# Windowed attention in blocks of 64 queries of two heads: narrower score products and a stacked mask product

## The chip, the core and the metric

The kernel runs on one core of a Trainium2 chip. The metric is device microseconds of one execution; the kernel before takes 908.87 us (median of 3 runs, 908.67 to 910.39). The profile is of a further execution, on the same core. Names of engines: TensorE (PE; its weight loads are PEld), VectorE (DVE), ScalarE (ACT), GpSimd (POOL) and SyncE (SP), which issues transfers.

## The reference

One layer of a decoder block on 1024 positions of width 1024: a normalized input goes through one projection whose columns feed an attention branch, a recurrent branch, two gate paths and two merge gates; both branches are gated, projected, merged, projected once more, added to the input and normalized. What the change touches is the attention: 16 heads of width 64, 4 heads per key and value head, each query seeing itself and the 127 positions before it, plus one learned sink per head.

```python
s = jnp.einsum('bnqkgd,bnskd->bnkgqs', qb, kb) * (1.0 / math.sqrt(hd))
diff = qi + BLOCK - kj                       # BLOCK = WINDOW = 128
band = (diff >= 0) & (diff < WINDOW)
s = jnp.where(mask[None, :, None, None], s, -1e30)
m = jnp.maximum(jnp.max(s, axis=-1, keepdims=True), sink)
p = jnp.exp(s - m)
denom = jnp.sum(p, axis=-1, keepdims=True) + jnp.exp(sink - m)
o = jnp.einsum('bnkgqs,bnskd->bnqkgd', p / denom, vb)
```

Everything is float32.

## The kernel before

Nearly all of its time is matmul. A float32 matrix is split into a high part (rounded to the format `F32R`, float32 in TensorE's faster reading) and a low part (the rest); a product is high by high, low by high and high by low, so three matmuls. The projection is done in seven quarter products per pair of output chunks (a Strassen scheme, `Pair` and `run`), and the products, their operand splits and what becomes of their results are put in an order written out by hand (`tc.manual_schedule`, the lists `fixed` and `waiting`, and the costs in tuples such as `("A", 0.62, 0, f1)`). No planner reorders anything: each engine and each queue of transfers runs in the order of the program. The costs in the tuples decide only where background steps are put, and the change leaves them as they are.

*Queries, keys, values.* The projections of queries and keys come out transposed (features on partitions, time along the free dimension), are rotated (`rope_a`) and split by `rope_b`: ScalarE casts the high part (L626), VectorE subtracts it (L630), and both go to memory (`q_d`, `k_d`), 512 positions at a time. `v_prep` reads values, and makes for each group of four heads two arrays: `vs_d`, the values, and `dv_d`, the values of a block of 128 positions minus those of the block before, each as high and low part side by side (128 columns).

*The attention stage* (the loop over u at L1626) goes through 32 blocks: 4 groups of 4 heads, 8 blocks of 128 queries each; block n = u % 8 of group g = u // 8. One iteration interleaves three blocks with pieces of other work (the last projections, then the recurrent branch's output projection, `rp_steps`):

- `scores(u)`: per head j two products of 256 key columns (128 for n = 0). The weights are the 128 queries of head j in `qs` (high part on 64 partitions, low on 64), the moving side the keys `ks` (high, then low): L1274.
- `maxima_a`, `maxima_d`: query row i may see keys i+1 to 127 of the earlier 128 and keys 0 to i of the later 128, which together are 128 places. ScalarE copies the later half (L1282), VectorE puts the earlier half over it where the mask `mgt` holds (L1288), and a maximum is taken (L1293) over 128 places and the sink, which GpSimd has put into column 128 (`sink`, L1262). For n = 0 GpSimd masks instead (L1291).
- `weights_a` and `weights_d` for block u-1: exponentials with sums (L1298), reciprocal and multiplication.
- `values(u-3)`: of a block's transposed probabilities, all go with `vs` of the block before, and what the mask leaves goes with `dv`. The high part `phc`, the low part `plc` and their masked copies `phm`, `plm` make four products of 512 columns (4 heads by 128 queries), two with `dv` alone for n = 0: L1346. `join_a` and `join_d` add the product with the values' high part and that with their low part (L1355 to L1367).
- `transposed(u-2)` (L1312), `split_a` (L1317) and `split_d` (L1323), then `masks(u-2)`: two selects by GpSimd over 4 heads by 128 queries (L1332).

`load_kq` brings keys and queries of two blocks on SP's queue, two pairs of blocks ahead, and waits there until the scores that used the buffer are done. `load_v` brings values of two blocks on GpSimd's queue. Behind the same SP queue stand the loads of gates (`ga_d`), of the recurrent branch's weights (`w_rp`) and states (`yh_d`, `yl_d`), and stores of its results (`tr_d`).

## Time and profile before

| What | Value |
|---|---|
| median of 3 runs | 908.87 us |
| profiled execution, its own time | 909.08 us |
| its span, first to last instruction | 907.4 us |
| granted TensorE clock, mean | 0.999 |
| TensorE busy, weight loads busy | 889.1 us, 739.2 us |
| VectorE, ScalarE, GpSimd busy | 725.8, 554.9, 124.7 us |
| attention stage, 560 to 735 us: TensorE, VectorE, ScalarE, GpSimd busy | 174.53, 153.55, 139.45, 77.34 us |
| transfers | 182.57 MB, 201 GB/s over the span |

Times in the tables of the profile are microseconds from the span's start unless marked ns. A row names the line of the kernel, the engine, the operation, and the tiles as out<-in; a matmul's busy time includes the tail in which the next one already runs, so the distance between starts says what one costs in a stream.

### The profile page before, as it was taken

What the parts mean: (1) busy time and instruction counts of PE and PEld (TensorE: products, weight loads), DVE (VectorE), ACT (ScalarE), POOL (GpSimd) and SP (SyncE); (2) the same over time, 40 slices, a digit from 0 to 9 for tenths busy, and PEclk for the clock granted to TensorE, in tenths of its full rate; (3) what the DMA queues carried; (4) which work ended last, traced back from release to release, by engine and by line L of the source; (5) the groups of instructions that cost most, each with busy time, mean ns of one, the idle gap of its engine ahead of it and who ended that gap; (6) DMA issues with size and microseconds to landing.
All of it is one profiled execution on the core that took longest, in us unless ns stands there. A gap on an engine that the chain in (4) does not pass through costs nothing.

```text
span 907.4 us, 12605 instructions
## 1 busy us (share of the span) xinstructions
PE 889.1 (98%) x4171; PEld 739.2 (81%) x4171; DVE 725.8 (80%) x1158; ACT 554.9 (61%) x1097; POOL 124.7 (14%) x204
## 2 busy tenths in 40 slices
PE   5999999999999999999999999999999999999997
PEld 3879888878888788878887888888888888888885
DVE  7988799698669974987698476899999846779875
ACT  6754675455556745774767685888888731114555
POOL 0120000000110000000100001354443421310002
PEclk9999999999999999999999999999999999999999
DMA  9951786862534360345345257996666258879314
GB/s 348 404 203 68 253 272 223 294 219 97 180 121 151 130 218 24 129 155 180 107 155 183 85 194 254 328 370 211 214 201 212 85 182 322 315 272 346 110 47 186
DMA packets 88882, 182.57 MB, mean 201 GB/s; under 512 B 14049, under 2 KB 30433, under 8 KB 88818
## 3 DMA queue, kind: packets, MB, share of 16 engines
q1 hardware_dynamic: 82192, 162.09, 51.8%
q0 software_dynamic: 6336, 19.37, 5.9%
q8 instruction: 33, 0.54, 0.3%
q10 hardware_dynamic: 290, 0.32, 0.1%
q14 instruction: 31, 0.25, 0.1%
HBM read 125.01 MB, written 57.12 MB: 201 GB/s over the span
## 4 chain that ended last, share of the span: by engine, by line
PE 86%; DVE 6%; DMA 3%; ACT 2%; issue 2%; SPq 0%; POOL 0%; DVEq 0%; ACTq 0%
PE bk L696 41%; PE rp L174 14%; PE bo L1857 7%; PE pmain L174 6%; PE pgate L992 5%; PE s_ps L1274 3%; PE pv L1346 3%; DMA r<-w_main 2%; PE pt L1312 2%; PE bk L174 1%; DVE wl L110 1%; PE bk L1520 1%; PE bk L1519 1%; PE bk L1518 1%; DMA wada<-w_ss 1%
## 5 line engine op out<-in xcount | busy, mean ns | idle before, releaser
L696 PE MATMUL bk<-nh,wl 128*128 128x512 f32 x368 | 143.9, 391 | 0.5 <-DVE wl L110 0.4
L696 PE MATMUL bk<-nh,wh 128*128 128x512 f32 x368 | 143.4, 390 | 0.0
L696 PE MATMUL bk<-nl,wh 128*128 128x512 f32 x368 | 143.2, 389 | 0.0
L696 PEld LDWEIGHTS bk<-nh,wl 128*128 128x128 f32 x368 | 69.1, 188 | 16.7 <-DVE wl L110 2.1
L696 PEld LDWEIGHTS bk<-nh,wh 128*128 128x128 f32 x368 | 69.1, 188 | 14.4 <-ACT rhi L626 0.2
L696 PEld LDWEIGHTS bk<-nl,wh 128*128 128x128 f32 x368 | 69.1, 188 | 14.4
L110 DVE TENSOR_TENSOR wl<-r,wh 128x512 fp32r<-128x512 f32 x112 | 80.1, 729 | 0.0
L60 POOL DMA_DIRECT2D wq_d<-wq x32 | 21.9, 685 | 407.2 <-DVE wq L1172 392.6
L104 ACT CAST wh<-r 128x512 fp32r<-128x512 f32 x112 | 68.0, 617 | 8.8 <-DMA r<-w_ap 5.1
L696 PE MATMUL bk<-hh,wh 128*128 128x512 f32 x184 | 71.6, 389 | 0.0
L696 PE MATMUL bk<-hh,wl 128*128 128x512 f32 x184 | 71.6, 389 | 0.0
L696 PE MATMUL bk<-hl,wh 128*128 128x512 f32 x184 | 71.6, 389 | 0.0
L110 DVE TENSOR_TENSOR wl<-ws,wh 128x512 fp32r<-128x512 f32 x80 | 54.8, 686 | 4.3 <-ACT wh L104 4.2
L104 ACT CAST wh<-ws 128x512 fp32r<-128x512 f32 x80 | 48.2, 614 | 3.3 <-PE bk L1520 2.7
L1298 ACT ACTIVATE p<-p,small 128x129 f32<-128x129 f32 x128 | 50.1, 401 | 0.0
L799 ACT ACTIVATE c<-bk 128x512 f32<-128x512 f32 x31 | 18.5, 595 | 44.0 <-PE bk L696 43.9
L696 PEld LDWEIGHTS bk<-hl,wh 128*128 128x128 f32 x184 | 34.5, 188 | 7.2
L696 PEld LDWEIGHTS bk<-hh,wl 128*128 128x128 f32 x184 | 34.5, 188 | 7.1
L696 PEld LDWEIGHTS bk<-hh,wh 128*128 128x128 f32 x184 | 34.5, 188 | 7.1
L1857 PE MATMUL bo<-wh,sum 128*128 128x512 f32 x128 | 39.6, 389 | 0.0
L1274 PE MATMUL s_ps<-ks,qs 128*128 128x256 f32 (+1 forms) x256 | 37.6, 289 | 0.0
L696 PE MATMUL bk<-hha,wl 128*128 128x512 f32 x92 | 36.1, 393 | 0.6 <-DVE wl L110 0.6
(409 smaller groups left out, 2290.1 us busy)
## 6 DMA issues: line engine op xcount, KB each, us to landing
r<-w_main SPq DMA_DIRECT2D x100, 256.0 KB, 4.3
wada<-w_ss SPq DMA_DIRECT2D x16, 512.5 KB, 9.3
qs<-q_d SPq DMA_DIRECT2D x16, 512.0 KB, 5.8
wq_d<-wq POOLq DMA_DIRECT2D x24, 256.0 KB, 2.8
wr<-wq_d SPq DMA_DIRECT2D x24, 256.0 KB, 5.0
ks<-k_d SPq DMA_DIRECT2D x24, 192.0 KB, 4.2
wq<-w_out POOLq DMA_DIRECT2D x16, 256.0 KB, 5.2
q_d<-rhi SPq DMA_DIRECT2D x16, 256.0 KB, 3.6
```

The lines of the kernel that those rows point to most:

```text
L60: return eng.dma_start(dst, src)
L104: A.copy(dst[0][:], src)
L110: V.tensor_tensor(out=dst[1][:], in0=src, in1=f32(dst[0][:]), op=ALU.subtract)
L174: mm = T.matmul(ps[hf], ww, xx[kc][hf], start=(kc == 0 and ww is w_h and xx is xh), stop=(kc == KC - 1 and xx is xl))
L696: W["pe"] = T.matmul(ps, ww[:, c], b[kc][xx_], start=(first and kc == 0 and i == 0), stop=(kc == 3 and i == 2), skip_group_check=not first)
L799: A.activation(t["t"], s(), AF.Tanh, scale=0.5)
L992: W["pe"] = T.matmul(ps[:, SL[hf]], ww[:, c0:c0 + P], xx_[:, SL[hf]], start=(ic == 0 and i == 0), stop=(ic == 1 and i == 2))
L1274: W["pe"] = T.matmul(o, qs[:, j, qc], ks[:, b, k0 + (0 if n else P):k0 + 256], start=(b == 0), stop=(b == 1))
L1298: A.activation(px[:, j, :], px[:, j, :], AF.Exp, bias=sm[:, 0, j:j + 1], accum_out=sm[:, 1, j:j + 1])
L1312: W["pe"] = T.transpose(pt[:, j, :], px[:, j, 0:P], ident[:])
L1346: W["pe"] = T.matmul(pv[:], b, m[:].rearrange("p j q -> p (j q)"), start=(i == 0), stop=(i == len(prods) - 1))
L1857: T.matmul(bank[p][i] if dst is None else dst, a[:, ts_], b[:][:, sl], start=(new and kc == 0 and j == 0), stop=(kc == 3 and j == 2), skip ...
```

## The change

A block of 128 queries of one head becomes two halves of 64 queries of two heads each.

- *Queries* are stored so that, within 256 positions, position 64 i + q stands at 4 q + i (`turned`, `natural`): the cast and the subtraction in `rope_b` read in the old order and write in the new one. Keys stay as they were.
- *Scores:* the weights of a product are the 64 queries of two heads (half h of the block, heads 0 and 1 or 2 and 3), every fourth element of `qs`; the moving side is the 192 keys that these queries can see (64 or 128 for n = 0). The mask compares within 64 columns, and the predicated copy covers 64 columns of each of four.
- *Values* are stored as 18 half blocks of 64 positions, the first two zero. `load_v` now runs per block, on SP's queue, and brings for each half its earlier 128 positions (`vb`) and the two differences (`vd`), in four transfers, three buffers deep.
- *The value products* take 256 columns each (one half of the queries): high and low probabilities with `vb`, and one product per half with `vd`, whose moving side `cm` holds the masked high part on partitions 0 to 63 and the masked low part on 64 to 127. For n = 0 only the second half has earlier keys.
- *Joins and sinks* follow the new order; the sinks come in two transfers, every second element. At the start GpSimd makes the smaller mask and zeroes the first two half blocks of the values with four transfers.

```diff
@@ -126,8 +126,8 @@
     cs4_d = tc.dram_tile([24, 4, S], F32, name="cs4_d")
     k_d = tc.dram_tile([512, S], F32, name="k_d")
     v_d = tc.dram_tile([P, 8, NG, 64], F32, name="v_d")
-    vs_d = [tc.dram_tile([P, 8, P], F32, name=f"vs_d{g}") for g in range(NG)]
-    dv_d = [tc.dram_tile([P, 8, P], F32, name=f"dv_d{g}") for g in range(NG)]
+    vs_d = [tc.dram_tile([18, 64, P], F32, name=f"vs_d{g}") for g in range(NG)]
+    dv_d = [tc.dram_tile([18, 64, P], F32, name=f"dv_d{g}") for g in range(NG)]
     gate_d = tc.dram_tile([1, D], F32, name="gate_d")
     q_d = [tc.dram_tile([512, S], F32, name=f"q_d{g}") for g in range(NG)]
     ga_d = [tc.dram_tile([2, P, S], F32, name=f"ga_d{g}") for g in range(NG)]
@@ -586,12 +586,18 @@
     ctab = rpp.tile([P, S], F32, name="ctab")
     stab = rpp.tile([64, S], F32, name="stab")
     G.memset(ctab[64:128, :], 1.0)
-    W["mgt"] = const.tile([P, P], U32, name="mgt")
+    W["mle"] = const.tile([P, 64], U32, name="mle")
     mf = rpp.tile([P, HALF], F32, tag="rh", name="mf", bufs=2)[:, :P]
-    G.memset(mf, 1.0)
-    G.affine_select(out=mf, in_=mf, pattern=[[1, P]], compare_op=ALU.is_gt, fill=0.0, base=0,
-                    channel_multiplier=-1)
-    G.tensor_copy(W["mgt"][:], mf)
+    G.memset(mf[:, 0:64], 1.0)
+    for e in range(2):
+        o = mf[64 * e:64 * e + 64, 0:64]
+        G.affine_select(out=o, in_=o, pattern=[[-1, 64]], compare_op=ALU.is_ge, fill=0.0, base=0,
+                        channel_multiplier=1)
+    G.tensor_copy(W["mle"][:], mf[:, 0:64])
+    zero = rpp.tile([P, HALF], F32, tag="rl", name="zero", bufs=2)
+    G.memset(zero[:, :P], 0.0)
+    for g in range(NG):
+        dma(vs_d[g][0:2].rearrange("i r c -> (i r) c"), zero[:, :P], G)
     for b in range(2):
         dma(ctab[b * 32:(b + 1) * 32, :], cs4_d[0:8].rearrange("f j t -> (f j) t"), G)
     dma(stab[0:32, :], cs4_d[16:24].rearrange("f j t -> (f j) t"), G)
@@ -599,6 +605,12 @@
 
     def blk(w=HALF):
         return stp.tile([P, HALF], F32, tag="c", name="c", bufs=5)[:, :w]
+
+    def turned(ap, on):
+        return ap.rearrange("p (b q i) -> p b i q", b=2, i=4) if on else ap
+
+    def natural(ap, on):
+        return ap.rearrange("p (b i q) -> p b i q", b=2, i=4) if on else ap
 
     def rope_a(src, th, dst):
 
@@ -619,15 +631,16 @@
             lambda: t["ra"], th, dst, 0)
 
     def rope_b(src, th, dst, r0=P):
-        t = {}
+        t, q = {}, dst is not k_d
 
         def f1():
             t["h"] = rpp.tile([P, HALF], F32R, tag="rh", name="rhi", bufs=2)
-            A.copy(t["h"][:], src())
+            A.copy(turned(t["h"][:], q), natural(src(), q))
 
         def f2():
             t["l"] = rpp.tile([P, HALF], F32R, tag="rl", name="rlo", bufs=2)
-            V.tensor_tensor(out=t["l"][:], in0=src(), in1=f32(t["h"][:]), op=ALU.subtract)
+            V.tensor_tensor(out=turned(t["l"][:], q), in0=natural(src(), q),
+                            in1=turned(f32(t["h"][:]), q), op=ALU.subtract)
             dma(dst[r0:r0 + P, SL[th]], t["h"][:])
             dma(dst[r0 + 2 * P:r0 + 3 * P, SL[th]], t["l"][:])
 
@@ -1211,7 +1224,7 @@
             for n_, d_, dst in (("v", "vs", vs_d), ("d", "dv", dv_d)):
                 V.tensor_tensor(out=t[d_][:, :, 64:128], in0=t[n_][:],
                                 in1=f32(t[d_][:, :, 0:64]), op=ALU.subtract)
-                dma(dst[g], t[d_][:])
+                dma(dst[g][2:].rearrange("(n b) r c -> (b r) n c", b=2), t[d_][:])
 
         waiting[1].extend(([] if g else [slots(4)]) + [
                            [("S", 0, 0, f0)], slots(4), [("D", 0, 0.85, f1)],
@@ -1227,10 +1240,13 @@
         psm_ctx.close()
         psx = pool(psx_ctx, "psx", space=PSUM)
         at = pool(at_ctx, "at", side="right")
-        W["sink"] = at.tile([P, NH], F32, name="sink")
+        W["sink"] = at.tile([P, NH // 2], F32, name="sink")
         fill_sink = sink(0)
         load_kq(0)
-        dma(W["sink"][:], rows[0:1, D:D + NH].to_broadcast([P, NH]))
+        sinks_ = rows[0:1, D:D + NH].rearrange("o (x e) -> o x e", e=2)
+        for e in range(2):
+            dma(W["sink"][64 * e:64 * e + 64, :],
+                sinks_[:, :, e].to_broadcast([64, NH // 2]))
         fill_sink()
         load_kq(1)
         load_v(0)
@@ -1246,32 +1262,36 @@
         dma(qs[:], q_d[g].rearrange("(a j) t -> a j t", j=4)[:, :, t0:t0 + 256])
         U["kq", m] = ks, qs
 
-    def load_v(m):
-        g, n0 = m // 4, (m % 4) * 2
-        vs = at.tile([P, 2, P], F32R, tag="vs", name="vs", bufs=2)
-        dv = at.tile([P, 2, P], F32R, tag="dv", name="dv", bufs=2)
-        dma(dv[:], dv_d[g][:, n0:n0 + 2, :], G)
-        lo = 0 if n0 else 1
-        dma(vs[:, lo:, :], vs_d[g][:, n0 - 1 + lo:n0 + 1, :], G)
-        U["v", m] = vs, dv
+    def load_v(u):
+        g, i0 = u // 8, u % 8 * 2
+        vb = at.tile([P, 2, P], F32R, tag="vb", name="vb", bufs=3)
+        vd = at.tile([P, 2, P], F32R, tag="vd", name="vd", bufs=3)
+        for e in range(2):
+            half = slice(64 * e, 64 * e + 64)
+            dma(vb[half], vs_d[g][i0 + e:i0 + e + 2].rearrange("i r c -> r i c"))
+            dma(vd[half], dv_d[g][i0 + 2:i0 + 4].rearrange("i r c -> r i c"))
+        U["v", u] = vb, vd
 
     def sink(u):
         px = at.tile([P, 4, P + 1], F32, tag="p", name="p", bufs=3)
         U["p", u] = px, at.tile([P, 2, 4], F32, tag="small", name="small", bufs=4)
-        gs = slice(u // 8 * 4, u // 8 * 4 + 4)
-        return lambda: G.tensor_copy(px[:, :, P:P + 1], W["sink"][:, gs].unsqueeze(2))
+        gs = W["sink"][:, u // 8 * 2:u // 8 * 2 + 2]
+        return lambda: G.tensor_copy(
+            px[:].rearrange("p (h a) k -> p h a k", h=2)[:, :, :, P],
+            gs.unsqueeze(1).to_broadcast([P, 2, 2]))
 
     def scores(u):
         g, n = u // 8, u % 8
         ks, qs = U["kq", u // 2]
-        qc = slice((n % 2) * P, (n % 2 + 1) * P)
-        k0 = (n % 2) * P
         s_full = psx.tile([P, 1024], F32, tag="s", name="s_ps")
         s_ps = s_full[:].rearrange("p (j k) -> p j k", j=4)
         for j in range(4):
-            o = s_ps[:, j, :] if n else s_ps[:, j, P:]
+            h = j // 2
+            t0 = (n % 2) * P + 64 * h
+            first = 0 if n else P - 64 * h
+            w = qs[:].rearrange("p j (q i) -> p (j q) i", i=4)[:, j % 2 * P:j % 2 * P + P, t0 // 64]
             for b in range(2):
-                W["pe"] = T.matmul(o, qs[:, j, qc], ks[:, b, k0 + (0 if n else P):k0 + 256],
+                W["pe"] = T.matmul(s_ps[:, j, first:192], w, ks[:, b, t0 + first:t0 + 192],
                                    start=(b == 0), stop=(b == 1))
         U["s", u] = s_ps, *U.pop(("p", u))
         if n % 2 and u // 2 + 2 < 16:
@@ -1279,17 +1299,25 @@
 
     def maxima_a(u):
         s_ps, px, sm = U["s", u]
-        A.copy(px[:, :, 0:P], s_ps[:, :, P:])
+        if u % 8:
+            A.copy(px[:, :, 0:P], s_ps[:, :, 0:P])
+        else:
+            A.copy(px[:, :, 0:64], s_ps[:, :, P:192])
+            A.copy(px[:, 2:4, 64:P], s_ps[:, 2:4, 64:P])
 
     def maxima_d(u):
         s_ps, px, sm = U["s", u]
-        p = px[:, :, 0:P]
+        p = px[:, :, 0:64]
         if u % 8:
-            V.copy_predicated(p, W["mgt"][:].unsqueeze(1).to_broadcast([P, 4, P]),
-                              s_ps[:, :, 0:P])
+            V.copy_predicated(p, W["mle"][:].unsqueeze(1).to_broadcast([P, 4, 64]),
+                              s_ps[:, :, P:192])
         else:
-            G.affine_select(out=p, in_=p, pattern=[[0, 4], [-1, P]], compare_op=ALU.is_ge,
-                            fill=-1e30, base=0, channel_multiplier=1)
+            G.memset(px[:, 0:2, 64:P], -1e30)
+            for e in range(2):
+                o = p[64 * e:64 * e + 64]
+                G.affine_select(out=o, in_=o, pattern=[[0, 4], [-1, 64]],
+                                compare_op=ALU.is_ge, fill=-1e30, base=0,
+                                channel_multiplier=1)
         V.tensor_reduce(out=sm[:, 0, :], in_=px[:], axis=AX.X, op=ALU.max, negate=True)
 
     def weights_a(u):
@@ -1324,36 +1352,33 @@
         U["m", u] = phc, plc
 
     def masks(u):
-        phc, plc = U["m", u]
-        ms = []
-        if u % 8:
-            for s_, tag in ((phc, "phm"), (plc, "plm")):
-                d_ = at.tile([P, 4, P], F32R, tag=tag, name=tag)
-                G.affine_select(out=d_[:], in_=f32(s_[:]), pattern=[[0, 4], [1, P]],
-                                compare_op=ALU.is_ge, fill=0.0, base=0,
-                                channel_multiplier=-1)
-                ms.append(d_)
-        U["m", u] = [phc, plc], ms
+        pieces = U["m", u]
+        cm = at.tile([P, 4, P], F32R, tag="cm", name="cm")
+        for i, s_ in enumerate(pieces):
+            G.affine_select(out=cm[64 * i:64 * i + 64].rearrange("p g (e q) -> p (g e) q", e=2),
+                            in_=f32(s_[0:64]).rearrange("p g (e q) -> p (g e) q", e=2),
+                            pattern=[[0, 8], [1, 64]], compare_op=ALU.is_ge, fill=0.0, base=0,
+                            channel_multiplier=-1)
+        U["m", u] = *pieces, cm
 
     def values(u):
-        n = u % 8
-        vs, dv = U["v", u // 2]
-        full, masked = U.pop(("m", u))
-        prods = [((vs if n else dv)[:, n % 2, :], m) for m in full]
-        prods += [(dv[:, n % 2, :], m) for m in masked]
-        pv = psx.tile([P, 4 * P], F32, tag="v", name="pv")
-        for i, (b, m) in enumerate(prods):
-            W["pe"] = T.matmul(pv[:], b, m[:].rearrange("p j q -> p (j q)"),
-                               start=(i == 0), stop=(i == len(prods) - 1))
-        U["pv", u] = [pv[:].rearrange("p (a e q) -> p a e q", a=2, e=2)]
-        if n % 2 == 0 and u // 2 + 1 < 16:
-            load_v(u // 2 + 1)
+        vb, vd = U.pop(("v", u))
+        phc, plc, cm = U.pop(("m", u))
+        pv = psx.tile([P, 4, P], F32, tag="v", name="pv")
+        prods = [(vb, m, h) for m in (phc, plc) for h in range(0 if u % 8 else 1, 2)]
+        prods += [(vd, cm, h) for h in range(2)]
+        for i, (b, m, h) in enumerate(prods):
+            js = slice(2 * h, 2 * h + 2)
+            W["pe"] = T.matmul(pv[:, js, :], b[:, h, :], m[:, js, :], start=(i == 0),
+                               stop=(i >= len(prods) - 2), skip_group_check=True)
+        U["pv", u] = [pv[:].rearrange("p (h a) (e q) -> p a e h q", h=2, e=2)]
 
     def join_a(u):
         pvv = U["pv", u][0]
         ob = at.tile([P, 2, P], F32, tag="ob", name="ob")
-        A.copy(ob[0:64], pvv[64:128, :, 0, :])
-        A.copy(ob[64:128], pvv[0:64, :, 1, :])
+        obv = ob[:].rearrange("p a (h q) -> p a h q", h=2)
+        A.copy(obv[0:64], pvv[64:128, :, 0])
+        A.copy(obv[64:128], pvv[0:64, :, 1])
         U["pv", u].append(ob)
 
     def join_d(u):
@@ -1362,9 +1387,10 @@
         if n % 2 == 0:
             W["yq"] = at.tile([P, 2, 256], F32, tag="yq", name="yq", bufs=3)
             U["yq", u // 2] = W["yq"]
-        yo = W["yq"][:, :, (n % 2) * P:(n % 2 + 1) * P]
-        V.tensor_tensor(out=yo[0:64], in0=pvv[0:64, :, 0, :], in1=ob[0:64], op=ALU.add)
-        V.tensor_tensor(out=yo[64:128], in0=pvv[64:128, :, 1, :], in1=ob[64:128], op=ALU.add)
+        yo = W["yq"][:, :, (n % 2) * P:(n % 2 + 1) * P].rearrange("p a (h q) -> p a h q", h=2)
+        obv = ob[:].rearrange("p a (h q) -> p a h q", h=2)
+        V.tensor_tensor(out=yo[0:64], in0=pvv[0:64, :, 0], in1=obv[0:64], op=ALU.add)
+        V.tensor_tensor(out=yo[64:128], in0=pvv[64:128, :, 1], in1=obv[64:128], op=ALU.add)
 
 
     yh, yl = [None] * KC, [None] * KC
@@ -1642,6 +1668,9 @@
         if u >= 3:
             values(u - 3)
             join_a(u - 3)
+        if 1 <= u < 32:
+            load_v(u)
+        if u >= 3:
             join_d(u - 3)
         if 2 <= u < 34:
             transposed(u - 2)
```

## The prediction

> **What bounds the kernel now.** I read the page first (span, engines, clock, chain), then the attention stage by windows, then single starts in the timeline.
>
> ```profile
> span 907.4 us, 12605 instructions
> PE 889.1 (98%) x4171; PEld 739.2 (81%) x4171; DVE 725.8 (80%) x1158; ACT 554.9 (61%) x1097; POOL 124.7 (14%) x204
> PEclk9999999999999999999999999999999999999999
> PE 86%; DVE 6%; DMA 3%; ACT 2%; issue 2%; SPq 0%; POOL 0%; DVEq 0%; ACTq 0%
> ...
> core 0: us, PE busy (x) PEld busy (x) DVE busy (x) ACT busy (x) POOL busy (x), PEclk, DMA share, GB/s
> 600.00:640.00 40.00, 40.00 (x223) 34.37 (x222) 38.12 (x69) 32.79 (x108) 18.88 (x32) 1.00 0.81 272
> ```
>
> TensorE is busy nearly throughout, at full granted clock, and 86% of the chain of waits is its own work. In the attention stage it never goes idle, but VectorE is busy 38.12 of 40 us beside it. So a change pays what it takes off TensorE's own sequence, as long as VectorE, ScalarE, GpSimd and SP's queue keep up. The busy time of a matmul covers its tail too, so I price by start-to-start distance:
>
> ```profile
> 68.25 0.28 PE L1518 MATMUL bk<-wh,hha 128*128 128x256 f32 x1
> ...
> 69.32 0.28 PE L1518 MATMUL bk<-wh,hha 128*128 128x256 f32 x1
> ...
> 554.75 0.39 PE L696 MATMUL bk<-hha,wh 128*128 128x512 f32 x1
> ...
> 559.96 0.39 PE L696 MATMUL bk<-nl,wh 128*128 128x512 f32 x1
> 560.19 1.00 PE L1274 MATMUL s_ps<-ks,qs 128*128 128x128 f32 x8
> 561.03 0.45 PE L696 MATMUL bk<-nh,wh 128*128 128x512 f32 x1
> 561.32 0.40 PE L696 MATMUL bk<-nh,wl 128*128 128x512 f32 x1
> ```
>
> Each of these matmuls brings new weights. 512 columns: 23 steps in 5.21 us, 0.2265 us each. 256 columns: 9 steps in 1.07 us, 0.119 us each. The slope is (0.2265 - 0.119)/256 = 0.42 ns per column, so a column count alone would give 0.065 us at 128 columns. Measured is more: from 560.19 to 561.32 stand eight products of 128 columns (the first block of a group) and one of 512, so the eight take 1.13 - 0.2265 = 0.90 us, 0.113 us each. That is a floor: below about 240 columns the load of the next 128x128 weights sets the distance, not the columns. The scores sit just above it.
>
> **The change part by part.**
>
> *Scores.* 8 products per block before, 8 after, with as many weight loads; 28 of the 32 blocks go from 256 to 192 columns, the 4 first blocks from 128 to 64 or 128.
>
> ```profile
> 641.65 0.60 PE L1312 MATMUL pt<-ident,p 128*128 128x128 f32 x4
> ...
> 645.78 0.39 PE L1346 MATMUL pv<-phc,vs 128*128 128x512 f32 x1
> ...
> 646.46 0.39 PE L1346 MATMUL pv<-plm,dv 128*128 128x512 f32 x1
> 646.70 0.60 PE L1312 MATMUL pt<-ident,p 128*128 128x128 f32 x4
> 647.05 1.19 PE L1274 MATMUL s_ps<-ks,qs 128*128 128x256 f32 x8
> 648.08 0.63 PE L174 MATMUL rp<-hha,wh 128*128 128x512 f32 x2
> ```
>
> From one block's transposes to the next's, 641.65 to 646.70, are 5.05 us. By the slope 192 columns would take 0.092 us, which lies under the floor of 0.113. So a product falls from 0.119 to 0.113: 28 x 8 x 0.006 = 1.3 us saved, not the 28 x 8 x 0.027 = 6.0 that the columns promise. The first blocks stay at the floor: nothing.
>
> *The stride.* A query tile now has its 64-query blocks interleaved by four, so the weights of a score product are 128 elements that lie four elements apart. No row shows a strided weight load. From below: the load as now, 0.113 us. From above: the load sweeps 2,048 bytes of each partition for its 512 bytes, and the nearest row that sweeps 2,048 bytes is the 512-column stream: 512 x 0.42 = 0.215 us of columns, 0.2265 with its fixed part. At 0.215 the scores cost 28 x 8 x (0.215 - 0.119) + 4 x 8 x (0.215 - 0.113) = 21.5 + 3.3 = 24.8 us more. I take the lower end for the sum, since count and shape of the loads are those of the row at 0.113, and keep the upper for the range. It is the dearest unknown here.
>
> [...]
>
> *Values.* In 28 blocks four products of 512 columns become six of 256. Rows above: 645.78 to 646.70 is 0.92 us for four; six at 0.119 with the same 0.01 before the transposes are 0.73. Saved 0.19 x 28 = 5.3 us. In the 4 first blocks two of 512 become four of 256: 4 x 0.119 - 2 x 0.2265 = +0.023 each, +0.1 us. These weights (values) are not strided.
>
> *Masks, softmax, joins.*
>
> ```profile
> 643.33 0.64 POOL L1332 TENSOR_SCALAR_AFFINE_SELECT phm<-phc 128x512 fp32r<-128x512 f32 x1 [0.82 <-ACT phc L1317]
> 644.86 0.96 POOL L1332 TENSOR_SCALAR_AFFINE_SELECT plm<-plc 128x512 fp32r<-128x512 f32 x1 [0.89 <-DVE plc L1323]
> ...
> L1288 DVE COPY_PREDICATED p<-mgt,s_ps 128x512 f32<-128x512 uint32 x28 | 20.7, 739 | 1.5 <-ACT p L1282 1.5
> L1367 DVE TENSOR_TENSOR yq<-pv,ob 64x256 f32<-64x256 f32 x32 | 13.7, 427 | 0.4
> ...
> 641.19 0.39 PE L1346 MATMUL pv<-phm,dv 128*128 128x512 f32 x1
> 641.19 0.19 PEld L1346 LDWEIGHTS pv<-plm,dv 128*128 128x128 f32 x1
> ...
>   POOL plm L1332: 0.6, 1
> ```
>
> The two selects keep 512 elements per partition, on 64 partitions, so I keep 0.64 and 0.96 (half that at best). The predicated copy halves to 256 elements: by the 256-element row about 0.43 for 0.74, 28 x 0.31 = 8.7 us less on VectorE, which is not the bound; it buys room. ScalarE's copy of scores, the exponentials, transposes and joins keep their element counts (in the 4 first blocks one more ScalarE copy and two smaller selects with a memset). Now the wait: the last mask before was done at 644.86 + 0.96 = 645.82. It is wanted when the fourth product's weights load, and a load goes out at the start of the product before it (the two rows at 641.19), here at 646.24 (645.78 + 2 x 0.23): 0.42 us spare, and once TensorE did wait 0.6 us for it (last row). After, both halves of the stacked mask are wanted when the fifth product's weights load, three steps of 0.119 in, and the values start 0.05 sooner: about 646.09, 0.27 us spare. I charge 1 us for stalls, from 0 to 28 x 0.1 = 3.
>
> *Value loads move from GpSimd's queue to SP's*, from 32 transfers to 128, and the bytes double (half blocks overlap).
>
> ```profile
> dv<-dv_d POOLq DMA_DIRECT2D x16, 128.0 KB, 5.3
> ...
> 643.23 1.24 SPq L60 DMA_DIRECT2D ks<-k_d  x2
> 644.52 0.60 SPq L60 DMA_DIRECT2D qs<-q_d  x1
> ...
> 655.30 1.04 SPq L60 DMA_DIRECT2D r<-w_rp  x2
> 672.97 0.62 ACT L104 CAST wh<-r 128x512 fp32r<-128x512 f32 x1
> ...
> SPq L60 <- PE s_ps L1274: 63.3, 13, 7.5
> ```
>
> An issue takes about 0.64 us of SP (two ks in 1.29, to the start of qs), so each block adds 4 x 0.64 = 2.6 us, behind a wait for the values of three blocks before (three buffers). Queued behind that wait are gate, weight and state loads of the next block. SP waited 63.3 us for the scores in this stage, so 32 x 2.6 = 82 us nearly fill it. The cover is earliness: w_rp loads issued at 655.30 are first cast at 672.97, and value loads have three blocks, 15 us, against 5.3 us to landing. I take 0; without that cover see the rivals.
>
> *Setup and rope.*
>
> ```profile
> L626 ACT CAST rhi<-c x13: 605/621/627, 98.2 to 192.2; 128x512 fp32r<-128x512 f32 x13
> L630 DVE TENSOR_TENSOR rlo<-c,rhi x13: 673/677/689, 99.5 to 195.0; 128x512 fp32r<-128x512 f32 x13
> 95.00:130.00 35.00, 35.00 (x156) 29.00 (x155) 30.09 (x50) 26.32 (x48) 0.00 (x0) 1.00 0.85 287
> ...
> 58.77 1.02 POOL L60 DMA_DIRECT2D ctab<-cs_d  x2
> 91.42 0.69 DVE L609 TENSOR_TENSOR c<-c,ctab 128x512 f32<-128x512 f32 x1
> ...
> L60 SPq DMA_DIRECT2D sink<-rows x1: 382/382/382, 552.9 to 552.9; - x1
> 562.85 0.69 DVE L1293 TENSOR_REDUCE small<-p 128x4 f32<-128x516 f32 x1 [5.40 <-POOL p L1291]
> ```
>
> Sixteen ScalarE casts and sixteen VectorE subtractions of queries write strided: between nothing and double, 16 x 0.68 = 11 us of VectorE. Between 95 and 130 us it has 5 of 35 us free while TensorE is full, so it stays hidden. Four zeroing transfers, a memset and an extra select delay the cosine table by about 3 us of GpSimd; issued at 58.77, it is first used at 91.42. The sinks come by element in two transfers instead of one; the first maximum at 562.85 waits for the mask, not for them, and 552.9 leaves 10 us. All 0.
>
> **Sum.** -1.3 (scores) -5.3 (values) +0.1 (first blocks) +1.0 (stalls) = -5.5 us. The profiled execution took 909.08 us (span 907.4 and 1.7 around it), 0.2 above the median 908.87. So 909.08 - 5.5 = 903.6, and against the median 903.4.
>
> **The rivals.**
>
> *A, strided weights are slow (it ends slower).* Place: the eight loads per block; price: 0.215 for 0.113. Then 24.8 - 5.3 + 0.1 = +19.6 us, 928.5; at 0.2265 a load, 256 x 0.0115 = 2.9 more, 931.4. It decides from 0.135 us a load on (5.5 us over 256 loads). For it: the load is already the limit here, so every nanosecond shows, and nothing in the trace reads 16 bytes per element at one element each 0.9 ns; the fastest stream takes four elements, 16 bytes, in 1.7 ns. Against it: that is no proof of a limit, and a load runs at half the stream's element rate anyway. [...]
>
> *B, the other queues take the gain.* With 2.6 us more issuing per 5 us block, behind a wait on TensorE, loads of the first ten blocks (the state rows besides) come late, or the mask is late each block. Price: 3 us of mask stalls and some 3 of late loads eat the 5.5 to nothing: about 908. For it: 38.12 of 40 us on VectorE and 0.27 us spare; against it: the relief of VectorE, the 17 us earliness above and GpSimd free of its transfers.
>
> *C, columns do pay:* were 0.113 a ramp and no floor, the scores would save 6.0, and the time is 898.7. The row at 128 columns speaks against it.
>
> **How the numbers follow.** Forecast 0.46 (901 to 906), A 0.42 (a part of it with loads between 0.135 and 0.215), B 0.09, C 0.03. The two big cases have opposite signs and turn on one price that the trace lacks, so the range must hold both: 900.5 to 931. A measurement of this kernel tells about 0.2%, 1.8 us, from no change: faster 0.49, same 0.08, slower 0.43.
>
> **What would show it.** In the changed profile: six value products 0.119 apart and eight score products 0.113 apart, start to start, in one block; right if both, and A if the scores stand near 0.2 while their load rows grow beyond what they are now. Idle time before the value products, ended by the mask or by VectorE, shows the 1 us too small; idle before weights casts ended by a transfer shows B. Casts of rotated queries at about 1.2 instead of 0.62 us would say that strides cost on ScalarE too, and make A likelier. The forecast is wrong if the scores' distance leaves 0.113 by more than 0.02.

## The result, and the profile after

| | before | after |
|---|---|---|
| median | 908.75 us | 942.25 us |
| profiled execution: span, granted clock | 907.4 us, 0.999 | 940.5 us, 0.993 |

The ratio is 1.0358, interval 1.0337 to 1.0378: 33.5 us slower, where 903.4 was forecast, and beyond the range's 931.

The page of the kernel after:

```profile
PE 915.4 (97%) x4235; PEld 771.1 (82%) x4235; DVE 728.0 (77%) x1158; ACT 562.9 (60%) x1101; POOL 115.5 (12%) x194
PEclk9999999999999999999999999998999999999999
PE 83%; DVE 5%; DMA 4%; ACT 3%; issue 2%; SPq 2%; POOL 0%; DVEq 0%; ACTq 0%; POOLq 0%
```

TensorE still sets the end, with 26.3 us more of its own work, and the clock now has a dent in one slice. The weight loads of the score products before, then after with the predicated copy (ns min/median/max, first and last start in us), and one block of the timeline after:

```profile
L1274 PEld LDWEIGHTS s_ps<-ks,qs x256: 186/189/192, 560.0 to 712.5; 128*128 128x128 f32 x128
```

```profile
L1294 PEld LDWEIGHTS s_ps<-ks,qs x256: 308/332/333, 559.3 to 746.5; 128*128 128x128 f32 x128
L1312 DVE COPY_PREDICATED p<-mle,s_ps x28: 448/456/467, 572.4 to 748.8; 128x256 f32<-128x256 uint32 x28
```

```profile
640.50 0.40 PE L1372 MATMUL pv<-phc,vb 128*128 128x256 f32 x2
...
640.98 0.40 PE L1372 MATMUL pv<-cm,vd 128*128 128x256 f32 x2
641.21 0.60 PE L1340 MATMUL pt<-ident,p 128*128 128x128 f32 x4
641.57 2.10 PE L1294 MATMUL s_ps<-ks,qs 128*128 128x192 f32 x8
643.51 0.65 PE L174 MATMUL rp<-yh,wh 128*128 128x512 f32 x2
```

Six value products go from 640.50 to 641.21: 0.71 us for 0.92 before. Eight score products take 641.57 to 643.51, the median distance of their starts being 0.235 us (0.119 before); their weights load for 332 ns (189 before). Scores: 28 x 8 x (0.235 - 0.119) + 4 x 8 x (0.235 - 0.113) = +29.9 us by the median distances. Values: -0.21 x 28 + 0.1 = -5.8.

The chain after, in order of time, and the waits that ended between 555 and 580 us (us in total, times, longest):

```profile
556.88 6.36 SPq L60
...
565.85 2.07 DMA vd<-dv_d
...
571.17 0.69 DVE wl L110
571.90 4.43 PE bk L709 x11
...
628.07 6.00 DMA qs<-q_d
```

```profile
POOL p L1279 <- DMA vd<-dv_d: 14.9, 1, 14.9
DVE small L1321 <- POOL p L1318: 13.8, 1, 13.8
PEld bk L709 <- DVE wl L110: 6.1, 1, 6.1
```

A stall that was not there before: TensorE's weight loads wait 6.1 us for VectorE's weights split (its products 5.8), VectorE stands at the first maximum for GpSimd's mask, and GpSimd stands at the copy of the sinks (L1279). The page puts that on a value load; the sink transfers, issued at 552.2 and 552.9, landed at 562.0 and 567.8, and the copy began at 567.9. SP was held too: the issue of the first value load behind the sinks took 6.36 us (the chain's `SPq`). After the stall eleven matmuls of 512 columns take 4.43 us, not 11 x 0.2265 = 2.49. The same by windows of the kernel after (busy of PE, PEld, DVE, ACT, POOL; then clock, DMA share, GB/s):

```profile
552.00:600.00 48.00, 42.25 (x194) 37.33 (x194) 24.94 (x48) 25.51 (x74) 10.43 (x23) 0.93 0.81 242
600.00:640.00 40.00, 38.56 (x190) 34.57 (x191) 32.20 (x59) 27.97 (x92) 14.85 (x25) 0.96 0.90 283
```

So +29.9 - 5.8 + 6.1 (stall) + 1.9 (matmuls after it) + 1.4 (idle at 634 us, scores waiting for `qs`) + 1.6 (slow matmuls after that, 3.71 us for ten and 2.09 for eight scores) = 35.1, against 33.1 between the spans: 2.0 too much. From a block's first score product to the product after its last, the 32 blocks together took 61.2 us where they took 32.3 before, so the scores cost 28.9 and not 29.9; the other 1.0 stays unplaced.

The rotated queries, written four elements apart:

```profile
L638 ACT CAST rhi<-c x13: 622/1128/1143, 97.2 to 191.5; 128x512 fp32r<-128x512 f32 x13
L642 DVE TENSOR_TENSOR rlo<-c,rhi x13: 672/1084/1105, 98.5 to 194.7; 128x512 fp32r<-128x512 f32 x13
```

### The profile page after: what moved, and what is told of

Read it like the earlier page. It is cut to its first block, busy times and chain, and to the rows that moved or that the text cites. A ratio compares the mean times of both kernels' runs of the same rounds, so it can differ in the third digit from the quotient of the medians.

```text
span 940.5 us, 13058 instructions
## 1 busy us (share of the span) xinstructions
PE 915.4 (97%) x4235; PEld 771.1 (82%) x4235; DVE 728.0 (77%) x1158; ACT 562.9 (60%) x1101; POOL 115.5 (12%) x194
## 4 chain that ended last, share of the span: by engine, by line
PE 83%; DVE 5%; DMA 4%; ACT 3%; issue 2%; SPq 2%; POOL 0%; DVEq 0%; ACTq 0%; POOLq 0%
PE bk L709 38%; PE rp L174 14%; PE bo L1886 7%; PE s_ps L1294 6%; PE pmain L174 6%; PE pgate L1005 5%; PE pv L1372 2%; DMA r<-w_main 2%; SPq L60 2%; PE pt L1340 1%; DVE wl L110 1%; PE bk L174 1%; DMA wada<-w_ss 1%; PE bk L1546 1%; PE bk L1545 1%
## 5 line engine op out<-in xcount | busy, mean ns | idle before, releaser
L709 PEld LDWEIGHTS bk<-nh,wh 128*128 128x128 f32 x368 | 69.6, 189 | 14.7 <-issue 0.2
L1294 PE MATMUL s_ps<-ks,qs 128*128 128x192 f32 (+2 forms) x256 | 66.4, 401 | 1.4 <-DMA qs<-q_d 1.4
L1294 PEld LDWEIGHTS s_ps<-ks,qs 128*128 128x128 f32 x256 | 62.4, 328 | 1.8 <-DVE yq L1393 1.6
```

The lines of the kernel that those rows point to most:

```text
L709: W["pe"] = T.matmul(ps, ww[:, c], b[kc][xx_], start=(first and kc == 0 and i == 0), stop=(kc == 3 and i == 2), skip_group_check=not first)
L1294: W["pe"] = T.matmul(s_ps[:, j, first:192], w, ks[:, b, t0 + first:t0 + 192], start=(b == 0), stop=(b == 1))
```

## The experiments

"Lost" in the expectations adds up by how much the distances between TensorE's starts exceed 0.227, 0.119 and 0.110 us for 512, 256 and fewer columns, counting only what exceeds them by over 0.06. Each kernel is compared with the kernel before on the same chip. Theory at the start: the stride of the score weights costs the 30 us (0.235 - 0.119 = 0.116 us a product, by the medians above), the sinks by element the 6.

**e4, the stride alone**: the kernel before, the weights of group g's score products read at every 2nd, 3rd, 4th or 8th element, so that its scores are those of other queries.

```diff
-T.matmul(o, qs[:, j, qc], ks[:, b, ...
+qw = qs[:].rearrange("p j t -> p (j t)")[:, 0:127 * st_ + 1:st_]   # st_ = (2, 3, 4, 8)[g]
+T.matmul(o, qw, ks[:, b, ...
```

> The kernel before, but the 128 weights of a score product are read from the same query tile at every 2nd, 3rd, 4th and 8th element in the four groups (so the scores are of wrong queries; everything else runs as before). It measures the price of a stride alone, with 256 columns. [...] Rival by bytes swept (the upper bound of the prediction): 0.119 at 2, 0.16 at 3, 0.215 at 4, 0.43 at 8. Second rival (any stride costs the same): 0.235 in all four. Time by the theory: 908.9 + 2 x 64 x 0.116 = 924 us and a few for the stride of 3.

One run, 928.4 us. The loads by group, and one chain entry from each:

```profile
L1277 PEld LDWEIGHTS s_ps<-ks,qs x59: 193/196/199, 560.8 to 592.4; 128*128 128x128 f32 x59
L1277 PEld LDWEIGHTS s_ps<-ks,qs x64: 251/261/264, 596.9 to 636.1; 128*128 128x128 f32 x64
L1277 PEld LDWEIGHTS s_ps<-ks,qs x62: 308/330/332, 640.8 to 683.3; 128*128 128x128 f32 x62
L1277 PEld LDWEIGHTS s_ps<-ks,qs x64: 312/342/345, 687.7 to 731.3; 128*128 128x128 f32 x64
```

```profile
576.65 0.97 PE s_ps L1277 x8
...
613.63 1.40 PE s_ps L1277 x8
...
658.55 1.87 PE s_ps L1277 x8
...
717.74 1.97 PE s_ps L1277 x8
```

Median distances 0.120, 0.174, 0.233 and 0.247 us. Beside these 256 columns, 0.119 us apart before, stride 2 is free, 3 is not, 4 costs twice and 8 hardly more than 4. The price follows neither bytes swept (8 would be twice 4) nor any stride at all (2 would cost). The sum in the expectation has 0.116 us more a product at 4 and 8; they took 0.114 and 0.128 more, and 3 took 0.055. What makes the price rise from 2 to 4 and hardly beyond was not shown.

**e2, the sinks as one row**, shared out by two GpSimd copies; the rest as after.

```diff
-            dma(W["sink"][64 * e:64 * e + 64, :], sinks_[:, :, e].to_broadcast([64, NH // 2]))
+        dma(sraw[:], rows[0:1, D:D + NH].to_broadcast([P, NH]))
+            G.tensor_copy(W["sink"][half, :], sraw[half].rearrange("p (x e) -> p x e", e=2)[:, :, e])
```

> The changed kernel, but the sinks come as one row for all partitions (64 bytes each, as before the change) and two small GpSimd copies sort them. Theory (the transfers of single sinks, 4 bytes each, hold up the queue and with it the first maximum, VectorE and the operand splits behind it): TensorE's 5.9 us of idle time at 571.9 goes, and most of the slow clock after it, some 7 us in all: about 935 us. Rival (the eight value and key transfers issued there do it): the idle time stays, about 942 us. The score products stay at 0.235 us.

936.15 us, 1.0294 (1.0269 to 1.0319). By windows the stall and the slow clock behind it are gone (the issue of the first value load takes SP 1.23 us there):

```profile
560.00:600.00 40.00, 39.96 (x196) 36.00 (x195) 25.00 (x49) 27.61 (x84) 12.96 (x29) 1.00 1.00 288
```

**e1, contiguous weights**: no interleaving; the query load sorts instead, in four transfers with runs of 64 elements. **e3**: the same with the sinks as a row.

```diff
-        dma(qs[:], q_d[g].rearrange("(a j) t -> a j t", j=4)[:, :, t0:t0 + 256])
+        for i in range(4):
+            dma(qs[:, i], q_d[g].rearrange("(a j) t -> a j t", j=4)[:, :, t0 + 64 * i:t0 + 64 * i + 64])
```

> The changed kernel, but queries are stored in their old order and the query load sorts them: four transfers per two blocks, in runs of 64, so that the 128 weights of a score product (64 queries of two heads) lie side by side. Theory (the stride of the weights sets the price of a score product): the products stand 0.113 us apart instead of 0.235, 256 x 0.122 = 31 us come back, about 911 us. Rival (the narrower columns, the 192-wide output or the new order of keys cost it, or the queues do): the distance stays near 0.235 and the time above 938 us. The casts of queries return to 0.62 us under both.

> Both edits together. Theory (these two prices are the whole error of the forecast): near the forecast of 903.4 us, 902 to 906. Rival (VectorE, GpSimd's masks or SP's queue take the gain of the values): 907 to 910 us, with idle time before the value products. A second rival: the query load in runs of 64 comes late and TensorE waits for it in every second block.

945.35 us, 1.0391 (1.0368 to 1.0413), and 936.43, 1.0299 (1.0271 to 1.0327). The weights load in 192 ns again, and the scores stand 0.112 apart, but TensorE goes idle; e1's score tile and a window:

```profile
L1295 PEld LDWEIGHTS s_ps<-ks,qs x256: 186/192/333, 559.7 to 748.6; 128*128 128x128 f32 x128
```

```profile
600.00:640.00 40.00, 30.14 (x162) 23.48 (x160) 25.94 (x50) 23.59 (x80) 13.02 (x22) 0.94 0.91 272
```

The distance is the theory's and the time the rival's: the remedy cost what it cured. SP never waits over 4 us in all for one cause from 555 to 720 us, being busy issuing, and scores wait for `qs` (8.2 us in e1, 6.1 in e3). In e3 the queries came late too, as its second rival said. A fair test needs a stride of 2, 0.120 us a product in e4, and an unchanged query load.

**e5, interleaved by two** within each block of 128, one load with runs of 2 KB, and the sinks as a row. **e6**: also the values stored with the half block inside the row (runs of 1 KB). **e7**: also the value loads issued by GpSimd.

```diff
-        w = qs[:].rearrange("p j (q i) -> p (j q) i", i=4)[:, j % 2 * P:j % 2 * P + P, t0 // 64]
+        w = qs[:, n % 2].rearrange("p j (q i) -> p (j q) i", i=2)[:, j % 2 * P:j % 2 * P + P, h]
```

> The changed kernel with the sinks as one row, and with queries interleaved by two within each block of 128 instead of by four within 256, stored block by block so that one transfer of 2 KB runs brings a pair of blocks: the weights of a score product are every second element, and SP issues no more than in the changed kernel. [...] Rival (128 value transfers on SP's queue are by themselves too many): loads of queries and values late, TensorE waits before scores and values as with the runs of 64, 915 us or more.

> As the one before, and values are stored with the half block inside the row, so that a value load moves runs of 1 KB instead of 512 bytes; count and queue of the transfers stay. Theory (the number of issues on SP counts, not the length of runs): the same time within 1 us. Rival (the transfer engines are the limit in the first 40 us of the stage): 2 to 4 us faster.

> As the one before, with the value loads issued by GpSimd, where they were before the change. Theory (SP's issues are what makes loads late): SP waits for TensorE again, no idle time before scores, and what the SP queue costs comes back; if the first of the three is already at 904, nothing changes. Rival (GpSimd's masks are the next bound): four issues of 0.55 us per block push the second mask select behind them, TensorE waits before the masked value products, 2 to 5 us slower than with SP.

919.63 us, 1.0123 (1.0105 to 1.0141); 918.65, 1.0111 (1.0094 to 1.0128); 919.66, 1.0124 (1.0106 to 1.0142). The chain of e5, two blocks in the later part:

```profile
643.37 0.93 PE s_ps L1300 x8
648.22 0.89 PE s_ps L1300 x8
```

Here a block takes 4.85 us where it took 5.05: the forecast's gain, 28 x 0.2 = 5.6. It is lost earlier: 14.7 us between 550 and 650 us, where the kernel before loses 1.8. e6 by windows:

```profile
600.00:640.00 40.00, 34.10 (x196) 28.94 (x194) 30.16 (x55) 26.09 (x84) 13.28 (x22) 0.96 0.92 286
640.00:680.00 40.00, 40.00 (x248) 35.84 (x247) 36.34 (x70) 34.10 (x111) 17.42 (x29) 1.00 0.81 244
```

Scores wait for `qs` from 555 to 650 us, 7.1 us in three times; run length is not why, since e6's longer runs took the same time as e5's. On GpSimd (e7) the queries come in time and the masks come late:

```profile
PEld pv L1380 <- POOL cm L1366: 7.1, 8, 2.1
```

Open by then: the bytes, the number of issues, or something else about the value loads.

**e8, whole tiles**: both value tensors stored once for each half of the partitions, so a block takes two transfers of 128 rows instead of four of 64, same bytes. **e9**: e6, loads for every second block only, so the blocks between are computed from wrong values. **e10**: e8 from GpSimd's queue. **e11**: e8, the second copy written by GpSimd. **e12**: e6, `vd` from GpSimd's queue.

```diff
-            dma(vb[half], vs_d[g][:, i0 + e:i0 + e + 2, :])
-            dma(vd[half], dv_d[g][:, i0 + 2:i0 + 4, :])
+        dma(vb[:], vs_d[g][:, i0:i0 + 2, :])
+        dma(vd[:], dv_d[g][:, i0 + 2:i0 + 4, :])
```

> The kernel with queries interleaved by two, sinks as a row and values stored with the half block inside the row, and in addition both value tensors stored once for each half of the partitions, so that a block's two value tiles come in two transfers of 128 KB where they came in four of 64 KB; the bytes are the same, the loads stay on SP's queue. Theory 1 (SP's queue is short of issues: the query load stands behind four value loads a block): the waits of the scores for qs in 560 to 640 us, 7.1 us in the kernel with four transfers, fall below 2 us, TensorE loses under 3 us there and the time is 905 to 910. Theory 2 (the 16 DMA engines are full there: their busy share was 0.95 and 0.92 in 560 to 600 and 600 to 640 us, 1.04 and 0.81 before the change, and the change doubles the value bytes, from 128 KB a block to 256): the waits stay above 5 us and the time is 916 to 920. The values are written twice to DRAM, up to 2 us more before 560 us in either case.

> The kernel with four value transfers a block, but values are loaded for every second block alone and the block after it uses the same tiles, so its outputs are computed from wrong values; as many issues on SP as with whole tiles, and half the bytes: 128 KB a block on the mean, as before the change. Theory 1 (issues): the same as with whole tiles, 905 to 910. Theory 2 (bytes): here alone the waits for qs fall below 2 us, and the time is 904 to 909, at least 7 us below that with whole tiles. If neither runs below 914, the value loads are not what delays the queries, and the rest (weights and rows for the products after it) is.

> As the kernel with whole value tiles, its two value loads a block issued by GpSimd, where the kernel before had two every second block. Theory 1: SP is free of them, and GpSimd issues two where four made the masks late by 7.1 us in all; masks wait under 3 us, no waits for qs, 903 to 908, the first version below the time before. Theory 2: waits for qs or for the weights of the products beside it stay, 914 to 920.

> As the kernel with whole value tiles loaded on SP's queue, but the second copy of the values (for the upper half of the partitions) is written to DRAM by GpSimd's queue, which issues nothing in 120 to 200 us; SP writes four transfers of 256 KB a group there, as in the kernel with four value loads a block, where it wrote eight. Theory 1 (the 17 us that TensorE lost in 136 to 226 us came from four more writes a group, some 0.9 us each, ahead of the weight loads on SP's queue): they shrink to the 2 to 3 us of the kernel with four value loads, the waits of the scores for qs stay below 1 us, and the time is 905 to 911, no slower than before by over 0.3%. Theory 2 (the bytes written are what delays the weight loads there, whichever queue issues them): TensorE still loses over 8 us in 120 to 230 us and the time is 916 to 924.

> The kernel with queries interleaved by two, sinks as a row and values stored once with the half block inside the row, whose four value loads of 64 KB a block are shared: the two of one tile stay on SP's queue, the two of the other go to GpSimd's. No value is written twice, so the 120 to 230 us stretch is as in the kernel with all four on SP (TensorE lost 2.6 us in 150 to 250 us). If the issues on one queue were what delayed the queries and, on GpSimd, the masks: both queues have two a block, as in the kernels with whole tiles, whose scores waited 0.7 and 0.9 us for qs and whose masks came 0.2 and 0.4 us late; TensorE loses 2 to 4 us in 550 to 650 us where it lost 13.7, and the time is 904 to 909, at or below the time before. If the 16 DMA engines are the limit there (the whole tiles had fewer and longer rows and a stage that began 15 us later), the waits for qs stay over 5 us and the time is 915 to 920.

| run | us | ratio (interval) | lost, 550 to 650 us |
|---|---|---|---|
| e8 | 926.29 | 1.0192 (1.0166 to 1.0217) | 2.5 |
| e9 | 909.90 | 1.0016 (0.9997 to 1.0036) | 6.6 |
| e10 | 930.20 | 1.0243 (1.0219 to 1.0267) | 3.5 |
| e11 | 927.10 | 1.0186 (1.0161 to 1.0211) | 3.6 |
| e12 | 916.59 | 1.0084 (1.0067 to 1.0100) | 9.8 |

e8's wait for `qs` falls to 0.7 us, yet it is slower, by an earlier window (the kernel before has 79.83 busy there):

```profile
120.00:200.00 80.00, 69.43 (x290) 56.31 (x289) 58.23 (x117) 38.23 (x68) 0.00 (x0) 0.94 0.83 249
```

Its doubled writes delay the weights there, whichever queue issues them (e11: 70.83), and e10 has the same writes, so the times of these three tell nothing of the attention stage. e12 has as many issues a queue as e8 and e10 have in all and still loses 9.8 us: the number of issues on a queue is not the limit. e9 halves both bytes and issues and can't part them.

**e13, values by pairs of blocks** (e6 with four transfers of 64 rows and 2 KB for two blocks, issued one pair ahead; SP). **e15**: the same on GpSimd. **e14**: the kernel before, each value load issued twice, the second into unused memory. **e16**: as e14, the second time in two transfers of 64 rows. **e17**: e5 with values stored as before the change and two loads of 128 rows a block from there, which are not the blocks that the products need, so its output is wrong.

```diff
+        dma(spare[:, 0], dv_d[g][:, n0:n0 + 2, :], G)             # e14; e16: per half of 64 rows
+        dma(spare[:, 1, lo:], vs_d[g][:, n0 - 1 + lo:n0 + 1, :], G)
```

> The kernel with queries interleaved by two, sinks as a row and values stored once with the half block inside the row; values are loaded for two blocks at a time, as before the change, in four transfers of 128 KB (64 rows of 2 KB) on SP's queue where it had eight of 64 KB. Bytes and writes are the same as with eight. If the number of transfers delays the queries: the waits of the scores for qs fall from 7.1 us to below 3, TensorE loses under 4 us in 550 to 650 us, and the time is 904 to 909. If the bytes do (128 KB a block more than before, 15 blocks in 85 us, 1.9 MB, at the 308 GB/s that the page shows there some 6 us): TensorE still loses over 7 us there and the time is 913 to 919.

> The kernel before, with each of its value loads issued a second time by GpSimd into memory that nothing reads: 256 KB a block where it had 128, as the change has, in two transfers more for two blocks; scores, sinks, masks and values are those of before. If the bytes delay the queries or the weights of the products beside them: TensorE loses over 4 us in 550 to 650 us, where it lost under 1, and the time is 913 to 918. If the number of issues on SP does, or if the queries and values of the changed kernel do in another way: no loss, 908 to 911, the same as before within 0.3%.

> As the kernel with value loads by pairs, its four transfers for two blocks issued by GpSimd, the queue that had two of them before. If the number of transfers and SP's queue are the limit: 903 to 908, as good as pairs on SP or better by up to 2 us, masks late by under 2 us in all. If the bytes are: 913 to 919, no better than pairs on SP.

> The kernel before, with each of its value loads issued again into memory that nothing reads, as in the run with the value bytes twice (911.4 us, TensorE lost 2.7 us in 550 to 650 us), but the second time in two transfers of 64 rows each, as the change loads its values; the same bytes, two more issues a block on GpSimd. If transfers to 64 partitions are what slows the 16 DMA engines: TensorE loses over 5 us in 550 to 650 us and the time is 914 to 920. If rows per transfer do not matter: 910 to 913; what GpSimd's two more issues cost shows as masks that come late, under 2 us.

> The kernel with queries interleaved by two and sinks as a row, with the values stored as before the change (128 partitions, one write of 512 KB a tensor and group) and each block's two value tiles loaded from there in one transfer of 128 rows each; the blocks are not the ones the products need, so the output is computed from wrong values. Bytes per block are those of the change (256 KB), issues on SP two a block, the stretch of 120 to 230 us is that of the kernel before. If 64-row transfers are the cause: waits for qs under 2 us in all, TensorE loses under 4 us in 550 to 650 us, and the time is 903 to 907, what the counted instructions give (5.3 us off the values). If the bytes at this point of SP's queue are: 912 to 918.

The transfers of 560 to 640 us by queue (packets, MB, share of the 16 engines' time), before, e14, e16, e17, e8, e6 and e13:

```profile
q1 hardware_dynamic: 13446, 20.98, 80.1%
q0 software_dynamic: 1264, 3.72, 12.2%
```

```profile
q1 hardware_dynamic: 13275, 20.72, 78.5%
q0 software_dynamic: 1881, 5.37, 19.4%
```

```profile
q1 hardware_dynamic: 12545, 19.86, 77.5%
q0 software_dynamic: 2096, 5.25, 19.4%
```

```profile
q1 hardware_dynamic: 15239, 24.38, 94.0%
q0 software_dynamic: 560, 1.84, 5.7%
```

```profile
q1 hardware_dynamic: 13711, 22.53, 85.5%
q0 software_dynamic: 848, 2.88, 9.3%
```

```profile
q1 hardware_dynamic: 13079, 21.12, 86.1%
q0 software_dynamic: 663, 2.19, 7.3%
```

```profile
q1 hardware_dynamic: 11472, 21.45, 91.2%
q0 software_dynamic: 636, 2.08, 6.7%
```

| run | value loads | us | ratio (interval) | engine share per MB |
|---|---|---|---|---|
| before | 128 rows | | | 92.3 / 24.70 = 3.74 |
| e14 | 128 rows, bytes twice | 911.39 | 1.0016 (1.0004 to 1.0029) | 97.9 / 26.09 = 3.75 |
| e16 | the second time 64 rows | 914.01 | 1.0057 (1.0042 to 1.0072) | 96.9 / 25.11 = 3.86 |
| e17 | 128 rows | 906.16 | 0.9972 (0.9960 to 0.9984) | 99.7 / 26.22 = 3.80 |
| e8 | 128 rows | 926.29 | 1.0192 (1.0166 to 1.0217) | 94.8 / 25.41 = 3.73 |
| e6 | 64 rows, 1 KB | 918.65 | 1.0111 (1.0094 to 1.0128) | 93.4 / 23.31 = 4.01 |
| e13 | 64 rows, 2 KB | 923.30 | 1.0169 (1.0135 to 1.0203) | 97.9 / 23.53 = 4.16 |
| e15 | 64 rows, 2 KB, GpSimd | 915.43 | 1.0064 (1.0044 to 1.0083) | 102.3 / 24.85 = 4.12 |

Doubled bytes alone cost 1.5 us by the ratio, and 64 rows instead of 128 some 3.7 more (e16 against e14, with two more issues for two blocks on GpSimd). e13 can't speak for the number of transfers: its products wait for the values themselves, 12.6 us in three times, which e6's do for 0.5, and its trace is of an execution of 929.29 us, 6 above its median. e17, with the same bytes as e6, takes 2.5 us less than the kernel before.

Over the changed kernels from e5 on, the share per MB parts by rows: 3.98 to 4.16 in the seven kernels that load all values by 64 rows (e5, e6, e7, e9, e12, e13, e15; four issues a block or two, on either queue), 3.71 to 3.80 in the five that load the change's bytes by 128 rows (e8, e10, e11, e17, e18). The first lose 6.6 to 20.2 us between 550 and 650 us, the second 2.5 to 5.9 (the stage of e8, e10 and e11 begins 17 to 20 us later). So rows are the likelier part. They are not the only difference: the 128-row kernels all have two issues a block, and an issue takes SP 0.34 us for 128 rows (e17) where it takes 0.58 for 64 (e6), medians. Of the 12.5 us between e6 and e17, 10.4 are lost in these 100 us (13.7 against 3.3); how they divide stays open.

**e18, the same with the right blocks**: e17, but GpSimd copies the values within DRAM into the doubled rows, 32 transfers.

```diff
+        if i_ >= n_steps * 45 // 100 and i_ % 2 and copies:
+            dma(dst[g][64 * e:64 * e + 64, f:f + 16, :] ..., src[g][64 * b:64 * b + 64], G)
```

> The kernel with queries interleaved by two, sinks as a row and whole value tiles of 128 rows, now with the blocks the products need: values are written to DRAM as before the change, and GpSimd's queue, between some 290 and 490 us, where the DMA engines' busy share was 0.35 to 0.44 and GpSimd does next to nothing, copies them within DRAM, 32 transfers of 256 KB, into rows stored once for each half of the partitions. If what the doubled writes cost (17 to 21 us in 130 to 230 us) came from their place, ahead of the weight loads of a stretch whose DMA share was already 0.70: nothing is lost before 550 us beyond what whole tiles with wrong blocks lost, and the time is 905 to 908, ratio 0.996 to 0.999. If the copies delay the weight loads where they now stand too: TensorE loses over 3 us in 290 to 490 us and the time is 909 to 915.

914.73 us, 1.0069 (1.0050 to 1.0088). GpSimd's queue stood behind other transfers and sent the copies in two bunches, 25 from 271 to 298 us and 7 from 445 to 451; weight splits came late after the first, and the stretch has 4.6 us more idle time than before (219.01 busy there):

```profile
280.00:500.00 220.00, 214.42 (x938) 175.59 (x939) 174.96 (x226) 145.12 (x208) 20.52 (x30) 1.00 0.49 169
```

Another 5.5 us were lost in 600 to 650 us (0.8 before). No kernel that computes the whole reference ran faster than the one before.

## Why the prediction was wrong

- *The stride* is the step that failed: I took "the lower end for the sum, since count and shape of the loads are those of the row at 0.113". A product took 0.235, above even the upper bound of 0.215 to 0.2265, which was worked out from bytes swept; the price does not follow these (e4: 0.233 at stride 4, 0.247 at 8). Rival A named the place; the cost was 28.9 us for its 24.8 to 27.7.
- *Sinks by element* were costed at nothing: "552.9 leaves 10 us". Landing took 9.9 and 14.9 us, not the 5.8 of the one row before, and cost 6.1 us (e2). The maximum waits for the mask, as said, but GpSimd makes the mask behind the copy of the sinks in its queue (562.16 behind 559.13 before the change), so late sinks are a late mask. The range ended at rival A without such a stall; this is over half of what lies beyond 931.
- *Value loads*, "I take 0": while the slow scores stretched the blocks, waiting for queries cost 3.0 us (1.4 idle, 1.6 slow products behind it); with fast scores much more is lost (13.7 us between 550 and 650 us in e6). The earliness was there, but from 560 to 640 us the 16 DMA engines have little room (92% busy before, 93% in e6, 100% in e17); price 12.5 us (e6 against e17). Rival B had this end, by SP's issues; the runs point to loads of 64 partitions without settling it (shares per MB of 3.98 to 4.16, for 3.71 to 3.80 with 128), and why such loads should cost more was not shown.
- *Scores' floor*, *values* and *first blocks* were right: 0.112 to 0.120 apart at stride 1 or 2, six value products in 0.71 us for 0.73 forecast, and e5's 4.85 us block. C falls: 64, 128 and 192 columns stood 0.118 to 0.120 apart in e5.
- *Stalls* of 1.0 for the mask did not come in the kernel after; TensorE's products waited over 1 us in all for masks only where GpSimd issued four value loads a block (e7, 5.4).
- *Rope*: the strided casts took 1.13 us for 0.62 and the subtractions 1.08 for 0.68, 1.8 and 1.6 times, and hidden as said: TensorE was busy 99.96 us between 100 and 200 us, where it was 99.83 before.

## What to carry to other kernels

Before interleaving a stationary operand, measure a product with weights at that stride: every second f32 cost little here (0.120 us a product for 0.112, e5 and e1), every fourth doubled the distance (0.235 for 0.119), and the load was the floor of a short product (0.118 to 0.120 at 64, 128 and 192 columns, e5). Where the DMA engines are nearly full (92% busy before, 100% in e17), prefer tiles loaded whole, over 128 partitions (3.71 to 3.80 of engine share per MB, for 3.98 to 4.16 over 64), and weigh a layout by what it does to its loads and writes (e8: TensorE busy 69.43 of 80 us, for 79.83) as well as to its products. A transfer by single 4-byte elements can hold up a stage (6.1 us, e2): bring the row and sort on chip.

## What was not expected of the hardware

- Weight loads by stride (f32, 128 x 128): 192 ns at 1 (e1), 196 at 2, 261 at 3, 330 at 4, 342 at 8 (e4).
- Two transfers of 64 x 8 single elements landed 9.9 and 14.9 us after issue; one of 128 rows of 64 bytes took 5.8 before the change and 7.7 in e2.
- With the wait of 6.1 us the granted clock stood at 0.93 over 552 to 600 us, the eleven matmuls after it taking 4.43 us for 2.49; without the wait it was 1.00 over 560 to 600 us (e2).
- The profile put the wait for the sinks on a value load; undoing the sinks (e2), not the row, told which it was.
